# Splitting a hand-written tick loop into a list of products and a list of attention heads

## The chip, the cores and the metric

The kernel runs on one core of a Trainium2 chip. The time is device microseconds (us) of one launch. The core has a matrix engine (TensorE, here PE), a vector engine (DVE), a scalar engine (ACT), GpSimd (POOL), a queue engine for transfers (SP), and eight PSUM banks into which PE writes. Each engine works through its own list of instructions in the order in which that list stands.

## The reference

The program is a stack of blocks in float32 on a sequence of 512 tokens with 1024 features. Cut to what the change touches:

```
for layer in (0, 1):
    x = x + 0.5 * swiglu_ffn(rms_norm(x))
    x = x + (even_mixer if layer == 0 else odd_mixer)(rms_norm(x))   # 16 attention heads each
    x = x + memory_cross_attention(rms_norm(x), rms_norm(mem))       # 4 heads of 256
    x = x + 0.5 * swiglu_ffn(rms_norm(x))
h = rms_norm(x); proj = h @ w_in                                      # the "second block"
y_a = (rg_lru(...) * gelu(...)) @ w_rnn_out
y_b = sparse_attention(q, k, v, ...) @ w_att_out                      # 16 heads
x = x + rms_norm((sigmoid(g_a) * y_a + sigmoid(g_b) * y_b) @ w_o)
x = x + rms_norm(swiglu(rms_norm(x)))
```

An attention head is `p = softmax(q k^T + bias)`, then `p v`. Every product with a weight is done as three matmuls of rounded parts (high by high, low by high, high by low), so every operand is first cut into a high part (a cast on ACT) and a low part (a subtraction on DVE).

## The kernel before

The stages run one after another: FFN, mixer, cross attention, FFN, twice, then the second block (recurrent part, attention, output, FFN). Within a mixer, a cross attention and the second block's attention, the code lists *ticks*. A tick is a pair: fills (products with weights: projections of q, k, v, gates, output units) and tasks (heads). Each fill and each head is a Python generator that issues some instructions and yields; one stretch between two yields is called a stage here. `Net.drive` walks the ticks: it starts the fills of the tick, steps every generator begun earlier by one stage, in the order in which they were begun, products and heads mixed, and starts the tick's heads. What has been issued first stands first in each engine's list, except that the scheduler beneath may let an instruction whose operands come later slip behind others. Nothing else sets the order here.

The stages:

- `tok_slow` (a product for q, k or v): 48 matmuls (L785 to L787), a yield, the other 48; `heads_alpha` then squares and sums on ACT and DVE and a small chain on POOL; after two further yields the scaled blocks are transposed (`spread`, L859) and evacuated (L851 on ACT, L852 on DVE). `values` writes the v parts (L879, L880).
- `heads` (a pair of heads): scores, 24 matmuls (L920) into six banks, with the row maxima (L944, DVE) and exponentials (L953, ACT) of both heads; then the division of the first head (POOL, L963); then nine or ten transposes of the first head into three banks (L974), each bank evacuated by a cast (L848, ACT) and a subtraction (L849, DVE); then p times v of the first head, eight matmuls (L982, L983), with the copy L992 (ACT) and the addition L993 (DVE), and the transposes of the second head; then p times v of the second head and the split of the pair (L514 ACT, L515 DVE).
- `gate_b` (second block only): 12 matmuls (L312 to L314), a yield, 12 more, then a multiplication (L1931, DVE), a tanh (L1932, ACT) and a transfer.
- weights: a transfer into one of two `raw` buffers, the cast `whi` (L306, ACT) and the subtraction `wlo` (L307, DVE) into one of four buffers each.

The ticks of the second block's attention, where q(g) is a projection, G(b) a gate and H(p) a pair of heads:

```
ticks = [([proj_k], []), ([q(0)], []), ([proj_v], []), ([], [])]
for h in range(16):
    x = [q(h // 4 + 1)] if h % 4 == 0 and h < 12 else [G(h // 2)] if h % 2 else []
    ticks.append((x, [] if h % 2 else [H(h // 2)]))
```

A pair of heads is begun every second tick and takes five, so two or three pairs are under way at a time, with a gate or a projection between them. In what follows "the scores of tick 2, 4, ..." are those of the pair begun in that tick of the loop.

Of the kernel before, what the change touches and what calls it, by code (L numbers as in the profile page):

```python
# [114 lines left out]
class Slot:  # L115
# [12 lines left out]
    @property  # L128
    def f(self):
        return self._get(F32)  # L130
# [44 lines left out]
class Net:  # L175
# [411 lines left out]


    def drive(self, ticks):
        act = []  # L590

        def start(f, into):
            g = f()
            if hasattr(g, "__next__"):
                step(g, into)

        def step(g, into):
            try:
                next(g)
                into.append(g)  # L600
            except StopIteration:
                pass

        i = 0
        while i < len(ticks) or act:
            fills, tasks = ticks[i] if i < len(ticks) else ((), ())
            i += 1
            new = []
            for f in fills:
                start(f, new)  # L610
            old = []
            for g in act:
                step(g, old)
            for f in tasks:
                start(f, new)
            act = old + new


    def ffn(self, nxt, wg, wu, wd, resid, tail=None, also=None):
# [1447 lines left out]
```

## Time and profile before

| | us |
|---|---|
| runs | 3235.32, 3234.91, 3226.97 (median 3234.91) |
| the profiled execution | 3229.99 |
| its span | 3228.2 |
| PE busy | 3134.5 (97%) |
| DVE busy | 2263.2 (70%) |
| ACT busy | 1600.1 (50%) |
| POOL busy | 343.2 (11%) |
| mean granted clock of PE | 0.983 of full speed |

The span is what the trace shows from the first to the last instruction; the profiled execution is one more launch, not one of the three runs. PE is busy nearly always, so time is to be had or lost only where PE waits, or where it works at the lower of its two clock levels (1.0 in the profile is 2.4 GHz, 0.5 is 1.2 GHz). In a timeline row, the number in brackets is how long the engine stood idle before the row, and behind the arrow stands the instruction whose end released it.

### The profile page before, as it was taken

What the parts mean: (1) busy time and instruction counts of PE and PEld (TensorE: products, weight loads), DVE (VectorE), ACT (ScalarE), POOL (GpSimd) and SP (SyncE); (2) the same over time, 40 slices, a digit from 0 to 9 for tenths busy, and PEclk for the clock granted to TensorE, in tenths of its full rate; (3) what the DMA queues carried; (4) which work ended last, traced back from release to release, by engine and by line L of the source; (5) the groups of instructions that cost most, each with busy time, mean ns of one, the idle gap of its engine ahead of it and who ended that gap; (6) DMA issues with size and microseconds to landing.
All of it is one profiled execution on the core that took longest, in us unless ns stands there. A gap on an engine that the chain in (4) does not pass through costs nothing.

```text
span 3228.2 us, 50963 instructions
## 1 busy us (share of the span) xinstructions
PE 3134.5 (97%) x20420; PEld 2822.7 (87%) x20420; DVE 2263.2 (70%) x3426; ACT 1600.1 (50%) x2686; POOL 343.2 (11%) x535
## 2 busy tenths in 40 slices
PE   8999999999999999999999999999999999989998
PEld 7999888798999989998897988999877887789997
DVE  8877566646777697775556557777679566578675
ACT  6544456555444364444456555444475265355444
POOL 1000123201000010001121110000211032210001
PEclk9999999999999999999999999999999999989999
DMA  4322211322233223222223322322312322413321
GB/s 159 113 94 85 93 52 56 121 92 88 85 104 100 99 96 108 94 86 85 92 73 104 118 80 82 107 94 85 102 60 91 99 82 66 160 53 105 105 92 66
DMA packets 104334, 300.81 MB, mean 93 GB/s; under 512 B 13856, under 2 KB 17440, under 8 KB 104096
## 3 DMA queue, kind: packets, MB, share of 16 engines
q1 hardware_dynamic: 94464, 287.74, 27.4%
q10 hardware_dynamic: 9632, 9.80, 1.0%
q8 instruction: 160, 2.62, 0.3%
q14 instruction: 78, 0.64, 0.1%
HBM read 291.21 MB, written 6.29 MB: 92 GB/s over the span
## 4 chain that ended last, share of the span: by engine, by line
PE 80%; DVE 10%; ACT 5%; issue 2%; DMA 2%; POOL 1%; ACTq 0%; SPq 0%; DVEq 0%; POOLq 0%
PE bank L312 19%; PE bank L313 19%; PE bank L314 19%; PE bank L785 4%; PE bank L786 4%; PE bank L787 4%; DVE wlo L307 2%; PE bank L1774 1%; PE bank L1775 1%; PE bank L1776 1%; ACT whi L306 1%; ACT slot L953 1%; PE bank L974 1%; DVE wlo L428 1%; PE bank L1155 1%
## 5 line engine op out<-in xcount | busy, mean ns | idle before, releaser
L312 PE MATMUL bank<-slot,whi 128*128 128x256 f32 (+1 forms) x2768 | 909.1, 330 | 15.6 <-ACT slot L514 6.5
L313 PE MATMUL bank<-slot,whi 128*128 128x256 f32 (+1 forms) x2768 | 912.3, 330 | 3.3 <-DVE slot L515 3.3
L314 PE MATMUL bank<-slot,wlo 128*128 128x256 f32 (+1 forms) x2768 | 910.5, 329 | 0.0
L427 ACT CAST whi<-fq 128x1024 fp32r<-128x1024 f32 x350 | 365.7, 1048 | 504.9 <-PE bank L313 402.4
L306 ACT CAST whi<-raw 128x1024 fp32r<-128x1024 f32 (+3 forms) x363 | 345.6, 954 | 526.1 <-PE bank L313 300.5
L312 PEld LDWEIGHTS bank<-slot,whi 128*128 128x128 f32 x2768 | 521.1, 188 | 68.7 <-ACT slot L514 8.3
L313 PEld LDWEIGHTS bank<-slot,whi 128*128 128x128 f32 x2768 | 521.5, 188 | 57.7 <-DVE slot L515 6.4
L314 PEld LDWEIGHTS bank<-slot,wlo 128*128 128x128 f32 x2768 | 523.1, 189 | 50.5
L307 DVE TENSOR_TENSOR wlo<-raw,whi 128x1024 fp32r<-128x1024 f32 (+3 forms) x363 | 410.4, 1132 | 215.6 <-ACT whi L306 212.9
L312 PE MATMUL bank<-gh,whi 128*128 128x256 f32 (+1 forms) x1712 | 541.2, 317 | 11.2 <-ACT whi L352 7.4
L314 PE MATMUL bank<-gh,wlo 128*128 128x256 f32 (+1 forms) x1712 | 536.8, 314 | 3.8 <-DVE wlo L353 2.9
L313 PE MATMUL bank<-gl,whi 128*128 128x256 f32 (+1 forms) x1712 | 537.8, 314 | 1.0 <-DVE gl L578 1.0
L428 DVE TENSOR_TENSOR wlo<-fq,whi 128x1024 fp32r<-128x1024 f32 x350 | 426.4, 1222 | 148.0 <-ACT whi L427 147.3
L312 PEld LDWEIGHTS bank<-gh,whi 128*128 128x128 f32 x1712 | 326.5, 191 | 37.1 <-ACT whi L352 8.1
L314 PEld LDWEIGHTS bank<-gh,wlo 128*128 128x128 f32 x1712 | 327.1, 191 | 26.1 <-DVE wlo L353 3.5
L313 PEld LDWEIGHTS bank<-gl,whi 128*128 128x128 f32 x1712 | 327.5, 191 | 24.0 <-DVE gl L578 2.3
L785 PE MATMUL bank<-whi,gh 128*128 128x256 f32 (+1 forms) x1056 | 302.4, 287 | 1.6 <-DVE slot L852 1.6
L786 PE MATMUL bank<-wlo,gh 128*128 128x256 f32 (+1 forms) x1056 | 300.0, 284 | 1.1 <-DVE wlo L307 0.9
L787 PE MATMUL bank<-whi,gl 128*128 128x256 f32 (+1 forms) x1056 | 299.8, 284 | 0.9 <-DVE gl L578 0.8
L172 POOL TENSOR_TENSOR sqacc<-sqacc,slot 128x512 f32<-128x512 f32 x62 | 100.8, 1626 | 1548.3 <-ACT slot L168 1547.4
L785 PEld LDWEIGHTS bank<-whi,gh 128*128 128x128 f32 x1056 | 201.3, 191 | 2.9 <-DVE slot L852 2.1
L786 PEld LDWEIGHTS bank<-wlo,gh 128*128 128x128 f32 x1056 | 201.1, 190 | 2.3 <-DVE wlo L307 2.0
(320 smaller groups left out, 4576.8 us busy)
## 6 DMA issues: line engine op xcount, KB each, us to landing
fq<-in_ffn_w_gu_dram SPq DMA_DIRECT2D x160, 512.0 KB, 3.3
raw<-in_ffn_w_down_dram SPq DMA_DIRECT2D x96, 384.0 KB, 3.1
raw<-in_w_in_dram SPq DMA_DIRECT2D x46, 512.0 KB, 3.4
raw<-in_xa_w_kv_dram SPq DMA_DIRECT2D x32, 512.0 KB, 3.6
raw<-in_od_w_in_dram SPq DMA_DIRECT2D x24, 512.0 KB, 3.5
raw<-in_w_ffn_down_dram SPq DMA_DIRECT2D x22, 512.0 KB, 3.5
fq<-in_w_ffn_gate_dram SPq DMA_DIRECT2D x40, 256.0 KB, 2.9
fq<-in_w_ffn_up_dram SPq DMA_DIRECT2D x40, 256.0 KB, 3.1
```

The costliest lines, as they stand in the source:

```text
L172: self.net.nc.gpsimd.tensor_add(self.parts[0], self.parts[0], sq)
L306: nc.scalar.copy(hi[:, :n], raw[:, :n])
L307: nc.vector.tensor_sub(lo[:, :n], raw[:, :n], hi[:, :n].bitcast(F32))
L312: mm(ps, wh, xh, start=start, stop=False, **k)
L313: mm(ps, wh, xl, start=False, stop=False, **k)
L314: mm(ps, wl, xh, start=False, stop=stop, **k)
L427: self.nc.scalar.copy(hi[:, :n], t[:, :n])
L428: self.nc.vector.tensor_sub(lo[:, :n], t[:, :n], hi[:, :n].bitcast(F32))
L785: mm(o, XH[k][:, t], wh, start=first, stop=False, skip_group_check=True)
L786: mm(o, XH[k][:, t], wl, start=False, stop=False, skip_group_check=True)
L787: mm(o, XL[k][:, t], wh, start=False, stop=last, skip_group_check=True)
L953: nc.scalar.activation(o, o, AF.Exp, bias=nm[:, i:i + 1], accum_out=den[:, i:i + 1])
```

## The change

`drive` keeps heads in `act` and products in `prod`. A tick now starts new products, then takes the begun products one stage further, then the begun heads one stage further, then starts new heads. Nothing is added and nothing is removed; every engine has the same instructions in another order.

```diff
     def drive(self, ticks):
-        act = []
+        act, prod = [], []
...
-        while i < len(ticks) or act:
+        while i < len(ticks) or act or prod:
             fills, tasks = ticks[i] if i < len(ticks) else ((), ())
             i += 1
-            new = []
+            new, further, old, begun = [], [], [], []
             for f in fills:
                 start(f, new)
-            old = []
+            for g in prod:
+                step(g, further)
             for g in act:
                 step(g, old)
             for f in tasks:
-                start(f, new)
-            act = old + new
+                start(f, begun)
+            act, prod = old + begun, further + new
```

The FFNs and the recurrent part run no heads and keep their order. Three places show what moves. Line numbers of the changed kernel are one higher from L617 on.

PE, second block's attention, tick 2, before: the last transposes of a head (L974, banks 26550 to 26552), then the second half of a gate (L312 to L314, bank 26463), then the scores (L920).

```order
L974 MATMUL bank_26551<-ident,slot_26429 128x128 x2
L974 MATMUL bank_26552<-ident,slot_26431 128x128
L974 MATMUL bank_26552<-ident,slot_26429 128x128
L312 MATMUL bank_26463<-gh_90,whi_26458 128x512
...
L314 MATMUL bank_26463<-gh_99,wlo_26459 128x512
L920 MATMUL bank_26595<-slot_26149,slot_26391 128x512
L920 MATMUL bank_26596<-slot_26149,slot_26391 128x512
```

The same place after the change, where the transposes write banks 26566 to 26568.

```order
L312 MATMUL bank_26463<-gh_90,whi_26458 128x512
...
L314 MATMUL bank_26463<-gh_99,wlo_26459 128x512
...
L975 MATMUL bank_26567<-ident,slot_26429 128x128 x2
L975 MATMUL bank_26568<-ident,slot_26431 128x128
L975 MATMUL bank_26568<-ident,slot_26429 128x128
L921 MATMUL bank_26595<-slot_26149,slot_26391 128x512
L921 MATMUL bank_26596<-slot_26149,slot_26391 128x512
```

The gate's half, twelve matmuls, moved from behind the transposes to ahead of them; the scores now stand right behind the transposes. It is so in ticks 2, 4 and 8, and in ticks 6 and 10 with a projection's second half and the p times v of a head in the row as well.

ACT, the same attention, tick 6, before: the copy and the split of a finished pair (L992, L514), the scaling of a projection (L1451), two weight casts (L306), the three casts of a head's transposes (L848), a third weight cast, the gate's tanh (L1932).

```order
L992 COPY slot_26946<-bank_26978 64x512
L514 CAST slot_26989<-slot_26946 128x512
L1451 ACTIVATE slot_27042<-bank_26729,nry_23949 128x256 x2
L306 CAST whi_27230<-raw_27229 128x1024
L306 CAST whi_27236<-raw_27235 128x1024
L1451 ACTIVATE slot_27045<-bank_26993,nry_23949 128x256 x2
L848 CAST slot_27065<-bank_27062 128x512
L848 CAST slot_27066<-bank_27063 128x512
L848 CAST slot_27067<-bank_27064 128x256
L306 CAST whi_27431<-raw_27430 128x1024
L1932 ACTIVATE slot_27103<-slot_27103 128x512
```

The same place after the change.

```order
L1452 ACTIVATE slot_27027<-bank_26729,nry_23949 128x256 x2
L306 CAST whi_27230<-raw_27229 128x1024
L306 CAST whi_27236<-raw_27235 128x1024
L1452 ACTIVATE slot_27030<-bank_26978,nry_23949 128x256 x2
L1933 ACTIVATE slot_27059<-slot_27059 128x512
L306 CAST whi_27431<-raw_27430 128x1024
L993 COPY slot_26946<-bank_27063 64x512
L514 CAST slot_27074<-slot_26946 128x512
L849 CAST slot_27081<-bank_27078 128x512
L849 CAST slot_27082<-bank_27079 128x512
L849 CAST slot_27083<-bank_27080 128x256
```

The three casts of the transposes are now last: the tanh, the third weight cast, the copy and the split of the pair stand ahead of them.

PE, odd mixer, 1579.7 us of the trace, before: the transposes of a head (banks 16085 to 16087), then the second half of a projection (48 matmuls, L785 to L787, bank 16114), and behind it the scores.

```order
L974 MATMUL bank_16086<-ident,slot_15888 128x128 x2
L974 MATMUL bank_16087<-ident,slot_15890 128x128
L974 MATMUL bank_16087<-ident,slot_15888 128x128
L785 MATMUL bank_16114<-whi_15917,gh_78 128x256
L786 MATMUL bank_16114<-wlo_15918,gh_78 128x256
L787 MATMUL bank_16114<-whi_15917,gl_79 128x256
```

The same place after the change, where the half product writes bank 16085 and the transposes write banks 16143 to 16145.

```order
L787 MATMUL bank_16085<-wlo_15924,gh_99 128x256
L788 MATMUL bank_16085<-whi_15923,gl_100 128x256
...
L975 MATMUL bank_16145<-ident,slot_15890 128x128
L975 MATMUL bank_16145<-ident,slot_15888 128x128
L921 MATMUL bank_16176<-slot_15694,slot_15782 128x512
L921 MATMUL bank_16177<-slot_15694,slot_15782 128x512
```

The half product stands ahead of the transposes, and the scores stand right behind them.

## Rows read from the trace of the kernel before

**Rows 1.** The page, parts 1 and 4: busy time by engine; chain by engine.

```profile
PE 3134.5 (97%) x20420; PEld 2822.7 (87%) x20420; DVE 2263.2 (70%) x3426; ACT 1600.1 (50%) x2686; POOL 343.2 (11%) x535
...
PE 80%; DVE 10%; ACT 5%; issue 2%; DMA 2%; POOL 1%; ACTq 0%; SPq 0%; DVEq 0%; POOLq 0%
```

**Rows 2.** Stages: window; length; PE, PEld, DVE, ACT, POOL busy; PE clock; DMA.

```profile
432.00:603.00 171.00, 162.40 (x1006) 140.01 (x1006) 106.70 (x231) 98.37 (x226) 44.10 (x89) 0.91 0.16 53
...
1557.00:1760.00 203.00, 188.38 (x1336) 172.74 (x1335) 126.00 (x307) 111.25 (x268) 43.06 (x107) 0.95 0.24 79
...
2595.00:2764.00 169.00, 160.19 (x1018) 138.07 (x1017) 103.46 (x265) 101.91 (x245) 47.63 (x102) 0.96 0.23 74
```

**Rows 3.** Timeline, PE: start, duration (us), line, operation, count [idle]; scores without a wait.

```profile
1586.89 2.19 PE L920 MATMUL bank<-slot,slot 64*128 64x512 f32 x24
2611.45 2.18 PE L920 MATMUL bank<-slot,slot 64*128 64x512 f32 x24
```

**Rows 4.** Timeline, PE: scores that waited inside for the evacuation of transposes.

```profile
1610.20 1.56 PE L920 MATMUL bank<-slot,slot 64*128 64x384 f32 x13 [1.14 <-DVE slot L849]
1632.55 1.31 PE L920 MATMUL bank<-slot,slot 64*128 64x384 f32 x10 [1.09 <-DVE slot L849]
2729.44 1.60 PE L920 MATMUL bank<-slot,slot 64*128 64x256 f32 x6 [1.03 <-DVE slot L849]
```

**Rows 5.** Timeline, ACT: a pair's split and three casts of transposes, odd mixer.

```profile
1608.08 0.62 ACT L514 CAST slot<-slot 128x512 fp32r<-128x512 f32 x1 [0.76 <-DVE slot L993]
1608.60 1.34 ACT L848 CAST slot<-bank 128x512 fp32r<-128x512 f32 x3
```

**Rows 6.** Timeline, DVE: the three subtractions that free the transposes' banks.

```profile
1609.45 1.62 DVE L849 TENSOR_TENSOR slot<-bank,slot 128x512 fp32r<-128x512 f32 x3
2610.07 1.62 DVE L849 TENSOR_TENSOR slot<-bank,slot 128x512 fp32r<-128x512 f32 x3
```

**Rows 7.** Timeline, ACT: weight cast and tanh in tick 2, second block.

```profile
2612.26 1.05 ACT L306 CAST whi<-raw 128x1024 fp32r<-128x1024 f32 x1 [1.54 <-DMA raw<-in_w_in_dram]
2613.22 0.63 ACT L1932 ACTIVATE slot<-slot 128x512 f32<-128x512 f32 x1
```

**Rows 8.** Timeline, PE: waits of heads and products that the new order may cover.

```profile
551.37 0.63 PE L859 MATMUL bank<-ident,slot 128*128 128x128 f32 x4 [2.89 <-DVE slot L841]
1701.70 0.38 PE L785 MATMUL bank<-whi,gh 128*128 128x256 f32 x1 [1.57 <-DVE slot L852]
2640.96 0.50 PE L982 MATMUL bank<-slot,vv 128*128 128x512 f32 x1 [1.43 <-ACT slot L848]
2701.82 0.50 PE L982 MATMUL bank<-slot,vv 128*128 128x512 f32 x1 [2.69 <-ACT slot L848]
```

**Rows 9.** Windows as in Rows 2: clock behind waits, and of twelve gate matmuls.

```profile
2595.00:2700.00 105.00, 100.88 (x727) 89.46 (x725) 67.06 (x180) 67.63 (x168) 34.91 (x79) 1.00 0.22 72
...
1634.10:1637.60 3.50, 3.50 (x16) 3.50 (x17) 3.50 (x18) 1.81 (x7) 0.00 (x0) 0.51 0.00 0
1614.00:1618.00 4.00, 4.00 (x38) 4.00 (x37) 2.09 (x10) 4.00 (x16) 1.67 (x4) 1.00 0.01 4
2702.50:2706.00 3.50, 3.50 (x18) 3.21 (x16) 2.24 (x4) 1.60 (x4) 0.48 (x2) 0.51 0.00 0
...
2711.90:2716.40 4.50, 4.50 (x16) 3.50 (x14) 3.85 (x19) 2.44 (x8) 0.00 (x0) 0.62 0.36 137
...
2718.70:2721.50 2.80, 2.80 (x14) 2.31 (x13) 1.48 (x3) 1.53 (x4) 2.66 (x6) 1.00 0.00 0
```

**Rows 10.** Timeline, PE, odd mixer: scores that waited for row maxima.

```profile
1668.22 1.01 PE L920 MATMUL bank<-slot,slot 64*128 64x256 f32 x3 [1.60 <-DVE mx L944]
```

**Rows 11.** Timeline, ACT, even mixer: a weight cast that waits for a product.

```profile
538.58 1.05 ACT L306 CAST whi<-raw 128x1024 fp32r<-128x1024 f32 x1 [2.52 <-PE bank L787]
```

**Rows 12.** Waits of PE in the first cross attention: total, times, longest (us).

```profile
PE bank L1381 <- POOL slot L1374: 2.7, 4, 1.1
...
PE bank L1322 <- DVE slot L852: 0.6, 2, 0.3
```

## The prediction

> **What bounds the kernel now.** I read the busy shares first. PE is busy 97% of the span and makes up 80% of the chain that ended last [rows 1]; none of the change's edits adds or removes an instruction. So the time can move in two ways only: where PE stands idle, and where its clock is at the lower level. I then took the windows of the stages that run heads [rows 2]. The reader is to see that PE is idle for about 9 us of 171 in the even mixer, 15 of 203 in the odd mixer and 9 of 169 in the second block's attention, and that its mean clock there is 0.91, 0.95 and 0.96. The rest of the program (FFNs, recurrent part) has the same order as before, and I give it zero.
>
> Last I looked at what ends each idle stretch. Scores need six of the eight PSUM banks. Where a weight product stands between a head's transposes and the scores, the scores run 2.2 us without a wait [rows 3]. Where they come right behind p times v and the transposes, they stop midway until a subtraction (L849) has freed a bank: 1.14, 1.09 and 1.03 us [rows 4]. The path behind such a stop is read in the odd mixer: the split of a finished pair waits 0.76 us for DVE, the three casts follow from 1608.60 [rows 5], the subtractions from 1609.45 to 1611.07 [rows 6], and the scores resume at 1610.20. The other idle stretches lie at heads' p times v (1.43 at 2640.96, a second one like it forty us later, 2.69 at 2701.82), at a projection (1.57) and at a projection's transposes (2.89) [rows 8].
>
> **The change, part by part.** In the second block, the gate's second half (twelve matmuls, 2.8 us [rows 9]) and projections' second halves move ahead of the heads' stages. That cover leaves the gap between transposes and scores and goes to the gap ahead of p times v or of the transposes.
>
> *Ticks 2, 4 and 8.* Before, in tick 2, the subtractions end at 2611.69 [rows 6] and the scores start at 2611.45 [rows 3], so there is nothing to wait for. After, the scores start at the same moment, but the transposes come 2.8 us later, and their evacuation with them. The nearest rows are the three stops of 1.0 to 1.1 us [rows 4], as the sequence on PE is then the same. ACT's list now has the gate's tanh, 0.63 us, among or ahead of these casts, and in tick 2 also a weight cast of 1.05 us that waits for its transfer until 2612.26 [rows 7]: the two casts behind it cannot end before 2613.31 plus two thirds of 1.34 [rows 5], and the last subtraction not before about 2614.7, where the scores ended at 2613.6. I take 1.1 + 0.6 = 1.7 for each, 5.1 together. Bounds: 0 (if two free banks were enough) and 2.8 each (the whole cover).
>
> *Ticks 6 and 10.* Here the tanh, a weight cast (1.05) and the pair's copy and split come ahead of the casts in ACT's list, and behind them wait the casts, the subtractions and so the scores: 1.1 + 0.6 + 1.05 = 2.8 each. Against that, the waits of 1.43 at p times v go [rows 8], since a projection's 48 matmuls and the gate's twelve now stand whole ahead of it. What is late next is the scores' bank, as said. Net 1.4 each, 2.8 together; bounds -1.4 and +2.8 each.
>
> *Tick 12.* Eight more gate matmuls, 8/12 of 2.8 = 1.9 us, come to stand in the 2.69 us wait [rows 8]: -1.9. The seven that stood ahead of this tick's scores are gone from there; the scores wait today already, and I add 1.0 (bounds 0 and 1.6, which is seven matmuls' time).
>
> The second block's waits come to 5.1 + 2.8 - 1.9 + 1.0 = +7.0 us.
>
> *Clock.* From 2595 to 2700, with all those scores unstopped, the granted clock is 1.00, that is 2.4 GHz [rows 9]. Behind the stop at 1632.55 PE ran at 0.51, near 1.2 GHz, from 1634.1 to 1637.6; behind that at 1610.20 it kept 1.00; behind the wait at 2701.82 it ran at 0.51 [rows 9]. Twelve gate matmuls take 4.4 us instead of 2.8 where such a stretch covers them [rows 9], 1.6 us more. Of the five new stops I let two be followed by such a stretch, +3.2; bounds 0 and 8.
>
> *Odd mixer.* At 1586.89 the scores had a projection's half ahead of them and no wait [rows 3]; now they follow the transposes: +1.1. Another such place is that at 1668.22, where the scores already wait 1.60 us for row maxima [rows 10]; with the transposes' banks also in use I add 1.1 (bounds 0 and 2.2). The wait of 1.57 ahead of a projection [rows 8] goes, because p times v and transposes no longer stand ahead of it: -1.6. One new stretch at the lower clock: +1.6 (bounds 0 and 3.2). Sum +2.2.
>
> *Even mixer.* A projection's second half moves ahead of a head's stages at 526 us. Its heads' scaling is then done earlier, and with it the wait of 2.89 us at 551.37 [rows 8] could go; but this evacuation still stands in DVE's list behind two earlier heads' additions and splits, and two weight casts, which wait 2.52 us for the product [rows 11], now stand ahead of a head's exponentials on ACT, with that head's sums behind them on PE. One end is -2.9 less 1.7 of clock, the other 2.52 + 1.05 = +3.6. I take +1, nearer the middle. On POOL the small multiplications of a projection pass ahead of a head's splits; they lie beside PE work.
>
> *Cross attentions.* K's transposes pass ahead of another head's p times v. The waits of 0.6 us on L852 may go, the 2.7 us on POOL's division [rows 12] stay, since POOL's work keeps its place. Bounds per layer -0.6 and +1.1 (one more wait of the longest kind); I take +0.25, +0.5 for both. SP's list of transfers is the same but for a few neighbours, as the weights' order hardly changes; I give it nothing, and it costs what tick 2 shows (a cast that waits for its transfer) if that is wrong.
>
> **The sum:** 7.0 + 3.2 + 2.2 + 1.0 + 0.5 = +13.9 us, made against the profiled execution of 3229.99, which gives 3243.9. That execution is 4.9 us below the median of the runs; on the median the sum gives 3248.8. I take the middle, 3247.
>
> **Rivals.** *First, faster: the cover pays and the stops don't come.* The moved products would then fill the waits at p times v (2 x 1.43 and 2.69), the projection's (1.57) and the transposes' (2.89), 10.0 us, and spare one or two stretches at the lower clock, 1.7 each: 12 us less, 3223. It decides at the evacuation: if the casts and subtractions keep up, so that a bank is free for each pair of score banks, the stops are nil. For it speaks that ACT is busy 50% [rows 1] and PE idles only for these waits; against it, that at all the places in this trace where scores follow transposes directly, they stop [rows 4].
>
> *Second, no difference: the waits only change place.* A tick's cover is the same 2.8 us, before or behind the transposes; what is lost at the scores is won at p times v, and the clock's stretches shift without growing. That gives 3235, give or take 6. For it: the waits at p times v are of the same size as the stops. Against it: there are three such waits in ticks 2 to 12, but five new stops.
>
> *Third, much slower: the clock.* Each of the seven new stops (five in the second block, two in the odd mixer) is followed by a stretch at the lower level. At 1.6 to 3.2 us each this is 11 to 22 us in place of the 4.8 in the sum: 3254 to 3265 on the median, say 3260. For it: the stops at 1632.55 and 2701.82 are followed so. Against it: that at 1610.20 is not.
>
> The Trainium skill bears on this rival: "TensorE: Matmul & The Clock Gate", section "A second HAM failure mode: psum-queue depth-cycling", describes a kernel that cycles through PSUM banks and whose PE idles briefly between groups of matmuls, so often that the clock swings between its levels. By that rule the third rival is the likely one, and the sum would be some 10 us more; the trace agrees at two stops of the three named, and with 1.00 where nothing stops.
>
> That the change doesn't do what it says can be left out: the order of PE's list shows the move at each place named.
>
> **How the numbers follow.** Forecast 0.50, first rival 0.17, second 0.20, third 0.13. A measurement of this kernel can tell about 0.3% (9.7 us) from no change, so faster means below 3225 and slower above 3245. The forecast's own bounds (no stop costs anything in ticks 6 and 10 and in the even mixer; or 2.8 at each stop) reach from about 3232 to 3262; of its 0.50, some 0.35 lie above 3245 and 0.15 within. All of the third rival is slower. Of the first, 0.12 lie below 3225 and 0.05 within; of the second, 0.16 lie within and 0.02 on either side. That makes 0.14 faster, 0.36 within, 0.50 slower. The range 3225 to 3264 leaves out most of the first rival and the top of the third.
>
> **What would show it.** Right: in the second block, scores of ticks 2, 4, 6, 8 and 10 with waits of 1 to 3 us on L850 (the subtraction's new line), the waits of 1.43 gone, that of 2.69 under 1, a clock below 1.00 in 2595 to 2700; in the odd mixer the wait of 1.57 gone and a new stop at the scores near 1587. Wrong: scores that run 2.2 us unstopped behind the transposes (first rival), or as much idle time as before in these windows (second). The even mixer is the weakest term, since its ends are 8 us apart.

## The result, and the profile after

| | before | after |
|---|---|---|
| median of five runs each, us | 3233.33 (3226.97 to 3235.32) | 3255.51 (3251.89 to 3264.8) |
| profiled execution, us | 3229.99 | 3251.89 |
| mean granted clock | 0.983 | 0.983 |

The ratio after to before is 1.0079, with a 95% interval of 1.0067 to 1.0091: the change makes the kernel slower, by 22 us between the medians and some 25 us by the ratio. The prediction was 3247, in a range of 3225 to 3264.

The page of the kernel after, parts 1 and 4, answers to [rows 1]:

```profile
PE 3135.7 (96%) x20420; PEld 2825.3 (87%) x20420; DVE 2266.4 (70%) x3426; ACT 1599.7 (49%) x2686; POOL 350.4 (11%) x535
...
PE 77%; DVE 12%; ACT 5%; DMA 3%; issue 2%; POOL 1%; ACTq 0%; SPq 0%; DVEq 0%; POOLq 0%
```

PE has the same work (3135.7 us busy against 3134.5), but the span is 21.9 us longer. In the chain, PE lost three points, and DVE has gained two and DMA one. So PE waits more, for DVE above all, and for transfers. The mean clock is 0.983 in both, so the clock takes about 55 us of either span: the 21.9 us of this execution are not the clock's.

The windows of the stages after, with the same columns as [rows 2]. Each window begins and ends at about the same matmuls as one of [rows 2].

```profile
433.50:603.60 170.10, 156.80 (x1006) 135.66 (x1006) 107.06 (x231) 98.18 (x226) 46.25 (x89) 0.94 0.16 53
...
1560.50:1774.00 213.50, 192.66 (x1336) 176.55 (x1336) 125.60 (x307) 111.43 (x268) 44.57 (x107) 0.94 0.23 76
...
2606.40:2782.10 175.70, 162.31 (x1017) 139.42 (x1016) 103.35 (x265) 101.68 (x244) 48.07 (x101) 0.96 0.22 70
```

The even mixer takes 170.1 us instead of 171.0, the odd mixer 213.5 instead of 203.0, the second block's attention 175.7 instead of 169.0. The second block went as forecast; the odd mixer did not.

PE in the second block's attention after, ticks 2, 4, 6, 8 and 10: first and last rows around each stop (L921 is the scores, L850 the subtraction that empties a bank of transposes, L994 the addition of a finished pair).

```profile
2622.81 2.18 PE L921 MATMUL bank<-slot,slot 64*128 64x512 f32 x24
2626.61 0.50 PE L312 MATMUL bank<-gh,whi 128*128 128x512 f32 x1 [1.62 <-DVE slot L850]
...
2646.34 0.38 PE L921 MATMUL bank<-slot,slot 64*128 64x256 f32 x1 [0.95 <-DVE slot L850]
2646.94 0.61 PE L921 MATMUL bank<-slot,slot 64*128 64x256 f32 x5 [0.22 <-DVE slot L850]
...
2667.78 0.38 PE L921 MATMUL bank<-slot,slot 64*128 64x256 f32 x1 [0.83 <-DVE slot L994]
2669.89 0.62 PE L921 MATMUL bank<-slot,slot 64*128 64x256 f32 x5 [1.72 <-DVE slot L850]
...
2690.24 0.38 PE L921 MATMUL bank<-slot,slot 64*128 64x256 f32 x1 [0.94 <-DVE slot L850]
2690.83 0.61 PE L921 MATMUL bank<-slot,slot 64*128 64x256 f32 x5 [0.22 <-DVE slot L850]
...
2710.19 0.38 PE L921 MATMUL bank<-slot,slot 64*128 64x256 f32 x1 [0.87 <-DVE slot L994]
2712.36 0.62 PE L921 MATMUL bank<-slot,slot 64*128 64x256 f32 x5 [1.79 <-DVE slot L850]
```

Where [rows 3] showed scores of 2.2 us without a wait, PE now stops at every one of the five: 1.62 us in tick 2 (not in the scores, but at the gate that follows, which waits for the last subtraction), then 1.17, 2.55, 1.16 and 2.66 us inside the scores. From the first score to the gate behind the scores the five places take 3.8, 3.9, 5.3, 3.9 and 5.4 us, where they took 2.1 each: 1.7, 1.7, 3.2, 1.7 and 3.3 us more.

ACT in tick 6 after shows why the stop is longest where the pair's copy and split stand ahead of the casts:

```profile
2663.67 0.63 ACT L1933 ACTIVATE slot<-slot 128x512 f32<-128x512 f32 x1 [1.73 <-DVE slot L1932]
2664.69 1.05 ACT L306 CAST whi<-raw 128x1024 fp32r<-128x1024 f32 x1 [0.39 <-DMA raw<-in_w_in_dram]
2665.77 0.58 ACT L993 COPY slot<-bank 64x512 f32<-64x512 f32 x1
2667.76 0.62 ACT L514 CAST slot<-slot 128x512 fp32r<-128x512 f32 x1 [1.42 <-DVE slot L994]
2668.29 1.34 ACT L849 CAST slot<-bank 128x512 fp32r<-128x512 f32 x3
```

The casts of the transposes (L849) cannot start before 2668.29, since ACT takes its list in order and waits 1.42 us at the split (L514) for DVE's addition. The addition itself (L994) runs on DVE only at 2667.04, behind the weight subtraction (L307) of the cast of 2664.69.

The odd mixer lost its time in a way the prediction doesn't have. PE and DVE after, around the pair whose scores ran freely at 1586.89 [rows 3]:

```profile
1592.47 1.61 PE L921 MATMUL bank<-slot,slot 64*128 64x384 f32 x13 [0.71 <-DVE slot L850]
...
1597.67 1.12 PE L860 MATMUL bank<-ident,slot 128*128 128x128 f32 x4 [3.01 <-DVE mx L945]
```

```profile
1596.91 0.69 DVE L945 CUSTOM_DVE_ANT_0 slot<-bank,slot 128x512 f32<-128x512 f32 x1 [3.18 <-DMA slot<-in_c_bias_o_dram]
```

The stop at the scores is there, with 0.71 us instead of the 1.1 forecast. But the row maxima (L945) then wait 3.18 us for the heads' bias, a transfer, and a projection's transposes (L860) wait 3.01 us for a bank behind them. Before, the same transposes waited for the row maxima too, but 1.28 us:

```profile
1590.36 0.44 PE L859 MATMUL bank<-ident,slot 128*128 128x128 f32 x2 [1.28 <-DVE mx L944]
```

So 1.73 us of the 3.01 are new. The bias is loaded by a transfer that stands in ACT's own list. ACT after, and then ACT before:

```profile
1587.70 1.05 ACT L306 CAST whi<-raw 128x1024 fp32r<-128x1024 f32 x1 [3.43 <-PE bank L788]
1589.11 1.05 ACT L306 CAST whi<-raw 128x1024 fp32r<-128x1024 f32 x1 [0.36 <-PE bank L788]
...
1591.86 0.34 ACTq L1122 DMA_DIRECT2D slot<-in_c_bias_o_dram  x1
```

```profile
1581.02 0.33 ACTq L1121 DMA_DIRECT2D slot<-in_c_bias_o_dram  x1
...
1585.58 1.05 ACT L306 CAST whi<-raw 128x1024 fp32r<-128x1024 f32 x1 [3.59 <-PE bank L787]
1586.99 1.05 ACT L306 CAST whi<-raw 128x1024 fp32r<-128x1024 f32 x1 [0.37 <-PE bank L787]
```

Before, the transfer was issued 5.9 us ahead of the scores (1581.02 and 1586.89), ahead of two weight casts. After, the product moved ahead of the heads took its casts with it; these wait 3.43 us for PE, and the transfer behind them goes out at 1591.86, when the scores are already running.

### The profile page after: what moved, and what is told of

Its sections match the earlier page's. It is cut to its first block, busy times and chain, and to the rows that moved or that the text cites. A ratio compares the mean times of both kernels' runs of the same rounds, so it can differ in the third digit from the quotient of the medians.

```text
span 3250.1 us, 50948 instructions
## 1 busy us (share of the span) xinstructions
PE 3135.7 (96%) x20420; PEld 2825.3 (87%) x20420; DVE 2266.4 (70%) x3426; ACT 1599.7 (49%) x2686; POOL 350.4 (11%) x535
## 4 chain that ended last, share of the span: by engine, by line
PE 77%; DVE 12%; ACT 5%; DMA 3%; issue 2%; POOL 1%; ACTq 0%; SPq 0%; DVEq 0%; POOLq 0%
PE bank L312 19%; PE bank L313 19%; PE bank L314 19%; PE bank L786 4%; PE bank L787 4%; PE bank L788 4%; DVE wlo L307 2%; ACT whi L306 1%; PE bank L1775 1%; PE bank L1776 1%; PE bank L1777 1%; DVE wlo L428 1%; PE bank L1156 1%; DVE slot L515 1%; DVE gl L578 1%
## 5 line engine op out<-in xcount | busy, mean ns | idle before, releaser
L312 PE MATMUL bank<-slot,whi 128*128 128x256 f32 (+1 forms) x2768 | 909.6, 330 | 15.5 <-ACT slot L514 6.5
L314 PE MATMUL bank<-slot,wlo 128*128 128x256 f32 (+1 forms) x2768 | 911.6, 329 | 0.0
L306 ACT CAST whi<-raw 128x1024 fp32r<-128x1024 f32 (+3 forms) x363 | 345.4, 953 | 537.8 <-PE bank L313 312.7
L312 PEld LDWEIGHTS bank<-slot,whi 128*128 128x128 f32 x2768 | 521.5, 189 | 68.2 <-ACT slot L514 7.9
L307 DVE TENSOR_TENSOR wlo<-raw,whi 128x1024 fp32r<-128x1024 f32 (+3 forms) x363 | 411.8, 1136 | 242.3 <-ACT whi L306 241.6
L314 PEld LDWEIGHTS bank<-slot,wlo 128*128 128x128 f32 x2768 | 523.1, 189 | 51.1
L312 PE MATMUL bank<-gh,whi 128*128 128x256 f32 (+1 forms) x1712 | 540.7, 317 | 14.5 <-ACT whi L352 8.0
L314 PE MATMUL bank<-gh,wlo 128*128 128x256 f32 (+1 forms) x1712 | 536.8, 314 | 3.9 <-DVE wlo L353 2.9
L312 PEld LDWEIGHTS bank<-gh,whi 128*128 128x128 f32 x1712 | 326.6, 191 | 40.6 <-ACT whi L352 8.7
L314 PEld LDWEIGHTS bank<-gh,wlo 128*128 128x128 f32 x1712 | 327.2, 191 | 26.3 <-DVE wlo L353 3.5
L787 PE MATMUL bank<-wlo,gh 128*128 128x256 f32 (+1 forms) x1056 | 302.9, 287 | 1.0 <-DVE wlo L307 0.9
L787 PEld LDWEIGHTS bank<-wlo,gh 128*128 128x128 f32 x1056 | 204.3, 193 | 2.0 <-DVE wlo L307 1.6
```

Of the source, the lines that this page charges most:

```text
L306: nc.scalar.copy(hi[:, :n], raw[:, :n])
L307: nc.vector.tensor_sub(lo[:, :n], raw[:, :n], hi[:, :n].bitcast(F32))
L312: mm(ps, wh, xh, start=start, stop=False, **k)
L314: mm(ps, wl, xh, start=False, stop=stop, **k)
L787: mm(o, XH[k][:, t], wl, start=False, stop=False, skip_group_check=True)
```

## The experiments

All kernels below are the kernel before with a `drive` that can do either order, so that each stage can be given one:

```diff
-    def drive(self, ticks):
-        act = []
+    def drive(self, ticks, mode="old"):
+        act, prod = [], []
...
             for f in fills:
-                start(f, new)
+                start(f, begun if mode == "old" else new)
+            for g in prod:
+                step(g, further)
             for g in act:
                 step(g, old)
```

Line numbers are some lines higher in them. A stage varies from one execution to the next, in part through the clock, so I give its length in two parts, both from the trace's clock records between the same two matmuls: what the clock took (length times one minus the mean granted clock) and the rest, the time at full clock. The trace columns below are time at full clock plus clock loss, in us, each from one execution.

| kernel | ratio to before (95%) | even mixer | odd mixer | second block's attention |
|---|---|---|---|---|
| before | | 155.5 + 15.4 | 196.9 + 10.2 | 151.5 + 6.8 |
| after | 1.0079 (1.0067 to 1.0091) | 159.7 + 10.2 | 203.8 + 13.7 | 158.1 + 6.8 |
| e_second | 1.0035 (1.0023 to 1.0047) | 155.5 + 18.8 | 200.1 + 6.8 | 157.3 + 11.9 |
| e_odd | 1.0042 (1.0030 to 1.0055) | 157.4 + 10.2 | 202.4 + 17.1 | 151.1 + 6.8 |
| e_evcr | 1.0014 (1.0003 to 1.0025) | 159.9 + 10.2 | 196.3 + 13.7 | 151.6 + 6.8 |
| e_gate | 1.0004 (0.9993 to 1.0015) | 156.4 + 13.7 | 201.8 + 10.2 | 146.5 + 5.1 |
| e_gate2 (the same kernel) | 0.9973 (0.9963 to 0.9984) | 155.4 + 18.8 | 197.6 + 11.9 | 146.6 + 5.1 |
| x_twice_new | no ratio, one execution | 157.3 + 10.2 | 198.7 + 11.9 | 166.1 + 15.4 |
| x_twice_gate | no ratio, one execution | 156.5 + 13.7 | 196.8 + 10.2 | 157.6 + 11.9 |
| x_early_new | 1.0018 (1.0008 to 1.0027) | 157.1 + 10.2 | 200.5 + 13.7 | 151.0 + 6.8 |
| e_oddonly | 0.9973 (0.9961 to 0.9984) | 156.4 + 13.7 | 194.1 + 6.8 | 151.6 + 6.8 |
| e_oddlate | 0.9957 (0.9941 to 0.9972) | 157.2 + 10.2 | 193.1 + 10.2 | 147.2 + 1.7 |
| e_best | 0.9956 (0.9943 to 0.9969) | 155.4 + 18.8 | 192.6 + 8.5 | 146.6 + 5.1 |
| e_late | 1.0020 (1.0007 to 1.0034) | 164.9 + 20.5 | 193.1 + 8.5 | 152.6 + 5.1 |

### Which stage loses it: the new order in one stage at a time

```diff
-        self.drive(ticks + [([B(0)], []), ([B(1)], [])])
+        self.drive(ticks + [([B(0)], []), ([B(1)], [])], mode="new")
```

(e_second; the same word at the odd mixer's `drive` for e_odd, and at those of the even mixer and the cross attentions for e_evcr.)

> Two lists only in the second block's attention, the old single list everywhere else. In the trace of the changed kernel that stage is 6.6 us longer than before. If the loss is made in the stage itself, by the scores' stops on the transposes' evacuation, this kernel is 6 to 8 us slower than the kernel before, with stops at the scores of ticks 2, 4, 6, 8 and 10 of 1 to 3 us and the waits of 1.43 us at p times v gone. If the stage only inherits something from the stages ahead of it (buffers, the phase of the clock), it is within 2 us of before.

> Two lists only in the odd mixer. In the trace of the changed kernel that stage is 10.4 us longer, where I had worked out 2.2. If that is the order's own doing (stops at the scores, and a projection's transposes that wait 3 us because their scaling stands behind row maxima in DVE's list), 8 to 12 us slower than before. If most of it came from an unlucky clock in that one execution, 2 to 5 us slower and a different placing of the half-clock stretches.

> Two lists in the even mixer and in both cross attentions, the old list in the odd mixer and the second block. The changed kernel's trace gives 0.6 us for the even mixer, 3.1 and 1.2 us for the two cross attentions. If these are the order's doing, 4 to 6 us slower than before, 2.5 of it at the first transposes of the first cross attention. If the first cross attention's wait there is chance, 1 to 3 us slower.

Measured: 1.0035, 1.0042 and 1.0014, that is about 11, 14 and 5 us; together 0.91%, against 0.79% for all at once, the same within the intervals. The stages lose by themselves; that one inherits anything from another is not seen. e_second and e_odd lost more than expected (6 to 8 and 8 to 12 us), though their intervals reach into these ranges; e_evcr's interval, 1 to 8 us, can't tell its two expectations apart. The waits of PE in the second block's attention of e_second (L925 is the scores, L854 the subtraction):

```profile
PE bank L925 <- DVE slot L854: 8.9, 8, 1.8
PE bank L925 <- DVE slot L998: 2.2, 2, 1.2
PE bank L312 <- DVE slot L854: 1.7, 1, 1.7
PE bank L988 <- DVE slot L854: 0.4, 1, 0.4
PE bank L987 <- ACT slot L853: 0.2, 1, 0.2
```

The scores' waits and the following gate's are 12.8 us in all, where the scores' were 3.2 before, and the waits at p times v are down from 5.5 us to 0.6. At full clock this stage is 5.8 us longer, in the kernel after 6.6; the other half of e_second's loss in this execution, 5.1 us, is the clock's. The odd mixer has 202.4 and 203.8 us in the new order; in the old one it varies between 196.3 and 201.8 over seven executions of this table (the first five kernels in the old order there, and both doubled ones), 198.3 in the mean. So its loss at full clock is 4.8 us between the means, give or take 2; the clock takes 15.4 in the mean instead of 10.7.

The first cross attention's 2.5 us were chance: e_evcr has the new order there, and its trace has that stage 0.6 us shorter than before, and the second one 3.3 us longer, as e_second has it with the old order. I take nothing of the cross attentions for shown.

### What makes the stops: gates back in the heads' list

```diff
+                start(f, begun if getattr(f, "gate", False) else new)
```

(Second block only: projections are products, gates keep their turn among the heads.)

> Old list everywhere but in the second block's attention, where only the projections go to the list of products and the gates stay in the list of heads, in the order in which they were begun. The projections' second halves then stand whole ahead of p times v, and the gates' halves stand between transposes and scores. If the stops come from the gates having left that place, the scores of ticks 2 to 10 run 2.2 us without a stop, the two waits of 1.43 us at p times v are covered, and the stage is 2 to 4 us shorter than before. If the moved projections make the stops, the stage is 3 to 6 us longer than before.

PE in e_gate, tick 6: p times v (L987) and the scores (L925).

```profile
2649.26 0.39 PE L987 MATMUL bank<-slot,vv 128*128 128x512 f32 x1
...
2654.51 2.21 PE L925 MATMUL bank<-slot,slot 64*128 64x512 f32 x24
```

```profile
PE bank L925 <- DVE slot L854: 2.0, 2, 1.0
```

Neither waits in tick 6: the projection's second half covers p times v, the gate's covers the evacuation. The whole stage has two waits left of scores for these subtractions, in ticks 12 and 14, where they stood before as well. It takes 146.5 us at full clock, 5.0 less than before, and the stops of ticks 2 to 10 are gone; the moved projections don't make them. The time was level, though, with the odd mixer 5 us longer in the old order. That was asked again:

> The kernel with the gates in the heads' list in the second block alone, once more: its first time was level with before (1.0004, 0.9993 to 1.0015) although its trace shows that stage 6.7 us shorter and the odd mixer, whose order is the old one, 5.0 us longer. If the odd mixer's 5 us were chance of one execution, the kernel is 3 to 8 us faster than before. If they come with the kernel in each execution, it is level with before again, and the odd mixer again takes over 210 us.

The second time the kernel is 0.27% faster, about 8.7 us, and the odd mixer takes 209.5 us. The attention's time at full clock is the same to 0.1 us in both (146.5, 146.6). Of the odd mixer's extra 4.9 us at full clock in the first trace, 2.3 are at a projection that waits 3.9 us, where it was 1.57 in [rows 8], and 1.6 at a head's transposes that wait for row maxima, in the same order. The two timings were made on different chips, each against the kernel before on the same chip; whether that is why one was level and the other not, and why one execution has these waits, stays open.

### The evacuation doubled

```diff
             self.evac(th[b][:, :n], tl[b][:, :n], tb[b][:, :n])
+            if getattr(self, "twice", False):
+                nc.vector.tensor_sub(tl[b][:, :n], tb[b][:, :n], th[b][:, :n].bitcast(F32))
```

> As the kernel with two lists in the second block's attention alone, and each subtraction that empties a bank of transposes is done twice there (32 heads' halves, three times about 0.54 us each, 1.62 us more DVE work per head; the result stays the same). If the stops at the scores are the wait for these subtractions, each stop of ticks 2 to 12 grows by 1 to 1.6 us, and the stage grows by 6 to 12 us over the 157.3 us at full clock of the kernel with two lists there. If DVE has room and the stops have another cause, the stage grows by less than 2 us.

> The same doubled subtractions in the kernel whose gates stay in the heads' list. With twelve gate matmuls (2.8 us) between transposes and scores, most of the extra 1.62 us should be hidden there in ticks 2 to 10: the scores stay without a stop or stop by less than 0.7 us, and the stage grows by 0 to 5 us over its 146.5 us at full clock, the rest of it in ticks 12 and 14. If the place of the gates is not what matters, it grows as much as the kernel with two lists does.

The waits of PE, first of the two lists with doubled subtractions (L983 is the second subtraction), then of the gates in the heads' list with them:

```profile
PE bank L925 <- DVE slot L983: 13.9, 6, 2.7
PE bank L312 <- DVE slot L983: 2.6, 1, 2.6
```

```profile
PE bank L925 <- DVE slot L983: 5.3, 4, 1.4
PE bank L925 <- DVE slot L1938: 3.0, 2, 1.5
PE bank L312 <- DVE slot L983: 1.6, 1, 1.6
```

With two lists the stage grows by 8.8 us at full clock (157.3 to 166.1), inside the expected 6 to 12, but not at each stop as expected: the stops of ticks 2, 4 and 8 grow by 0.9 to 1.1 us, those of ticks 6, 10 and 12 don't grow (2.5, 2.6 and 1.6 us, against 2.7, 3.0 and 1.5 in e_second), and that of tick 14 grows by 1.2; some 4 us of the growth are waits at p times v. So in ticks 2, 4 and 8 the stop is the wait for these subtractions; in ticks 6 and 10, where the copy, addition and split of a pair stand ahead of the casts, doubling them doesn't show it. The second expectation missed: with the gates in between the stage grows by 11.1 us (146.5 to 157.6), and PE, which had no stop there in ticks 2 to 10, now stops for 1.2 to 1.6 us. By the words of the expectation that speaks against the gates' place. But the gates' place is worth 8.5 us with the subtractions doubled (166.1 against 157.6) and 10.8 without (157.3 against 146.5). A reading that fits both is that the gate's 2.8 us are not more cover than the evacuation needs but just as much; [rows 6] and [rows 3] agree, with subtractions that end at 2611.69 and scores that start at 2611.45. In ticks 4 and 8 of this kernel the scores wait for the gate's own multiplication (L1938), which now stands behind the doubled subtractions on DVE.

### The bias transfer

```diff
         def heads(p):
             st["po", p] = []
-            bt = [self.vbias(a["c_bias_o"][2 * p + x], 512) for x in range(2)]
+            bias_of(p)
+            bt = st["bt", p]
+            bias_of(p + 1)
```

(`bias_of` loads the bias of a pair unless it has been loaded.)

> Two lists in the odd mixer alone, and the bias of a pair of heads is loaded two ticks earlier, when the pair before it begins, so that its transfer no longer stands behind a product's weight casts in ACT's list. In the changed kernel's trace that transfer is issued at 1591.9 us and the row maxima wait for it 3.18 us, a projection's transposes 3.01 us behind them. If that is a part of the odd mixer's loss, the wait of the row maxima at the second pair is gone, the odd mixer's time at full clock falls from 202 to 204 us to 198 to 201, and the stops of 1 to 1.7 us at the scores stay. If the row maxima would have been late in any case, it stays at 202 or more.

The row maxima of the second pair (L953 on DVE) and PE's transposes behind the scores in x_early_new:

```profile
1590.80 0.68 DVE L953 CUSTOM_DVE_ANT_0 slot<-bank,slot 128x512 f32<-128x512 f32 x1
```

```profile
1589.62 1.61 PE L929 MATMUL bank<-slot,slot 64*128 64x384 f32 x13 [0.71 <-DVE slot L858]
1591.16 1.09 PE L868 MATMUL bank<-ident,slot 128*128 128x128 f32 x8
```

No wait for the transfer is left, the transposes follow the scores at once, and the stop of 0.71 us at the scores stays. So the transfer's place makes these waits. How much of the loss that is, is less sure: the stage takes 200.5 us at full clock, 1.9 to 3.3 less than with the late transfer, which would be about half of the 4.8 lost, but one execution of the same order differs from another by up to 5.5 (196.3 to 201.8). The ratio falls from 1.0042 to 1.0018, but the two were timed on different chips, and e_gate and e_gate2 differ by as much in the same order. The rest of the loss, with the scores' stops and the clock, was not taken apart further.

### Faster than both

If cover between transposes and scores is what counts, a new product's first half, 48 matmuls, can give it in the odd mixer: further products, further heads, new products, new heads.

```diff
-            for f in fills:
-                start(f, new)
             for g in prod:
                 step(g, further)
             for g in act:
                 step(g, old)
+            for f in fills:
+                start(f, new)
             for f in tasks:
                 start(f, begun)
```

> A try to beat both: in the second block's attention projections in the list of products and gates in the heads' list; in the odd mixer a tick of further products, further heads, new products, new heads, so that a new product's 48 matmuls stand between transposes and scores. If cover at that place is what counts, the odd mixer's time at full clock falls from 196 to 202 us to about 192, the second block's attention stays near 146.5, and the kernel is 5 to 10 us faster than before. If the products are then late for the heads that need them, the odd mixer is no shorter, and the kernel is within 5 us of before.

> Only the odd mixer with new products behind further heads and ahead of new heads, everything else in the old order. The faster version changed two stages at once; its trace gives 3.7 us for the odd mixer (207.1 to 203.4) and 9.5 for the second block's attention (158.4 to 148.9). If the gains are the stages' own, this kernel is 2 to 8 us faster than before. If only both together gain, it is within 2 us of before.

The scores of the second pair in e_oddlate, where both kernels had a wait in or behind them:

```profile
1583.88 2.20 PE L929 MATMUL bank<-slot,slot 64*128 64x512 f32 x24
```

This version takes 3217.58 us, 0.9957 of the kernel before (0.9941 to 0.9972), some 14 us less. The odd mixer alone gives 0.9973; its time at full clock is 193.1 us in this version and 194.1 alone, below all seven executions in the old order. The scores of the odd mixer alone, before and in e_oddlate (window around the whole mixer, its length, PE busy with scores, count, clock, DMA), then two waits of PE at p times v (L991) in e_oddlate:

```profile
1498.20:1780.20 282.00, 26.81 (x192) 0.96 0.27 89
```

```profile
1493.90:1772.40 278.50, 20.27 (x192) 0.96 0.27 90
```

```profile
PE bank L991 <- DVE slot L1002: 3.0, 2, 1.9
PE bank L991 <- DVE hss L827: 2.5, 1, 2.5
```

With their waits (8.8 us before, 4.1 in e_oddlate) the scores take 11.2 us less, so the cover does what it was meant to do there. The stage gains only 3.8 of it at full clock, since p times v now waits 6.6 us instead of 0.7. With the early bias on top:

> The faster version (gates in the heads' list in the second block, new products ahead of new heads in the odd mixer) with the early bias. If the bias transfer also holds up row maxima there (3.6 us in one place of its trace), the odd mixer falls from 193.1 us at full clock to 189 to 192 and the kernel is 14 to 18 us faster than before; if it only moves the wait, 11 to 14 us as without it.

It is 0.9956, about 14 us faster: the odd mixer's 192.6 us are only 0.5 below 193.1, so in that order these runs show no cost of the transfer.

The same rule carried to the even mixer, and to the second block (its projections, and its gates, which begin there behind the heads' further stages), does harm:

> New products behind further heads and ahead of new heads in the even mixer, the odd mixer and the second block's attention (gates in the heads' list there). In the second block this also puts a projection's first half between transposes and scores in ticks 4, 8 and 12. If cover behind the transposes is what counts, as fast as the try with the odd mixer alone or up to 4 us faster. If starting new products late delays the weights' casts and transfers, 3 to 8 us slower than that try.

The ratio is 1.0020, some 20 us slower than e_oddlate, where 3 to 8 were expected. The even mixer takes 164.9 us at full clock and the second block's attention 152.6, 7.7 and 5.4 more than in e_oddlate. Waits of PE in the even mixer of e_late:

```profile
PE bank L991 <- ACT slot L857: 9.5, 3, 4.8
PE bank L983 <- POOL slot L972: 4.1, 2, 3.4
PE bank L868 <- DVE slot L850: 3.1, 2, 2.9
```

Heads wait at p times v (L991) for the casts of transposes, 9.5 us against 4.0 in the kernel after, and at transposes (L983) for POOL's division. That this comes of the new product, which no longer stands ahead of the heads' next stage, fits the order, but was not tried by itself.

## Why the prediction was right, and where it was off

*The second block's stops: right.* Predicted 1.7 us in ticks 2, 4 and 8 and 2.8 in ticks 6 and 10; the idle rows show 1.62, 1.17, 1.16 and 2.55, 2.66, and the five places are 1.7 and 3.2 to 3.3 us longer. The waits of 1.43 us and the 2.69 us of [rows 8] are gone. Only tick 12 was off: its scores stop 1.54 us, but stopped 1.46 (1.15 and 0.31) before, so the 1.0 added there is 0.1. The sum of waits was +7.0; at full clock the stage grew by 6.6, and by 5.8 in e_second. That the place of the gates makes or removes all five stops (e_gate), and the length of the evacuation moves those of ticks 2, 4 and 8 (x_twice_new), shows the mechanism.

*The clock: not borne out.* +4.8 was allowed in all; over the whole span the clock took about 55 us before and after. For the second block +3.2 was allowed for two stretches. The kernel after has two behind the new stops, but loses others, so that the stage's loss stayed at 6.8 us; in e_second it grew by 5.1. For the odd mixer +1.6; it was 3.5 and 6.9. The even mixer's clock took 5.2 less. Stops of the same size were followed by a stretch at 1.2 GHz in one execution and not in another: in e_second, with the same order in this stage, the granted clock falls behind the stops of ticks 2, 8 and 10 (0.61, 0.63 and 0.50) and stays at 1.00 behind those of ticks 4 and 6. The third rival, by which each stop brings one, didn't come: the kernel's mean clock is 0.983 before and after. The Trainium skill's "TensorE: Matmul & The Clock Gate", section "A second HAM failure mode: psum-queue depth-cycling", read as a rule, made it the likely course. The traces agree only so far that a stop can bring such a stretch: in the kernel after, behind the stops of ticks 4 and 10 the granted clock is 0.63 (2647.3 to 2651.9 us) and 0.57 (2713 to 2717 us), behind those of ticks 2, 6 and 8 it stays at 1.00. Where the stops are 2.2 to 2.6 us each, in x_twice_new, it falls behind all five (0.63 to 0.68), in the one execution there is.

*The odd mixer: the term that was too small.* Predicted +2.2, measured +10.4, of it 6.9 at full clock in the kernel after (4.8 between the means of the two orders). Three steps failed. The number of stops was short: two of 1.1 us were added, but the waits of PE for the subtraction, first before and then after, went from three to six and by 4.2 us:

```profile
PE bank L920 <- DVE slot L849: 3.0, 3, 1.1
```

```profile
PE bank L921 <- DVE slot L850: 7.2, 6, 1.7
```

The step on queues said of SP's list that it hardly changes, and looked at no other list with transfers; but the heads' bias goes out from ACT's list, behind the moved product's weight casts: the wait is 3.18 us on DVE and 3.01 on PE, 1.73 more than before, and behind it the granted clock is 0.50 (1598.0 to 1601.5 us). The wait of 1.57 us that was to go came back at another projection as 1.86 us:

```profile
1693.46 0.39 PE L786 MATMUL bank<-whi,gh 128*128 128x256 f32 x1 [1.86 <-DVE slot L994]
```

*The even mixer: near in its length by luck.* Predicted +1; between the same matmuls the trace gives about -1, as 4.2 us more at full clock and 5.2 less lost to the clock. (The 0.6 us named with e_evcr come from a window that began 1.5 us too early in the order after.) At full clock both executions in the new order (159.7, 159.9) lie above all in the old (155.4 to 157.4), by 3.4 us between the means, near the upper end of +3.6. PE's waits grew from 8.4 to 13.1 us, at p times v from 2.0 to 4.0, and a head's sums (L1186), which had no wait, wait 1.8 us; what makes them was not tried. The wait of 2.89 us that might have gone stayed:

```profile
554.10 1.08 PE L860 MATMUL bank<-ident,slot 128*128 128x128 f32 x4 [3.19 <-DVE slot L842]
```

It was said to be held by the earlier heads' additions and splits on DVE; that it did not shrink agrees, but was not tried by itself.

*The cross attentions:* +0.5 predicted; the execution after has +3.1 and +1.2, but e_evcr, with the new order, has -0.6 and +3.3, as e_second has with the old one. Nothing is shown.

*The total.* The sum of 13.9 us had 4.8 of clock in it and 9.1 of all else. What came in the profiled execution was 21.9 us, with less than 1 of clock. The second block was understood; that the other terms, with the even mixer's and the clock's errors against each other, left the time inside the range was partly luck. That it was slower by more than forecast is above all the odd mixer's doing.

*The first rival* (faster) named its condition rightly: with evacuation covered, the waits at p times v are a gain. e_gate is that kernel, 5.0 us shorter at full clock, and the change as made isn't.

## What to carry to other kernels

Work that stands between a head's transposes and the next user of their banks covers the evacuation: here twelve matmuls, 2.8 us, were just enough. Moved elsewhere they paid for one wait and opened another, which was larger in sum. When work is split into lists by kind, follow the transfers too, on every engine that issues them: here a load in ACT's list came late behind another product's weight casts, which waited 3.43 us. One rule for all stages was worse here than a rule for each.

## What was not expected of the hardware

Stages whose instruction order is the same differ between executions by more than the clock explains: the odd mixer's time at full clock lay between 196.3 and 201.8 us in the old order, while the second block's attention repeated to 0.6 us (151.0 to 151.6). The same kernel, timed twice against the kernel before, on two chips, gave 1.0004 and 0.9973, outside each other's intervals. A difference of 0.3% between two such timings is thus no finding here. That holds for e_oddonly's 0.27% as well, which was timed once; the 0.43 and 0.44% of e_oddlate and e_best come from two chips.
